# Moving TensorE's operands by 32 bytes, onto multiples of 256 bytes

## The chip, the core and the metric

The kernel runs on one core of a Trainium2 chip. A core has a matrix engine (TensorE, PE in the profile, with its weight loads shown apart as PEld), a vector engine (VectorE, DVE), a scalar engine (ScalarE, ACT), a general one (GpSimd, POOL), and a queue engine that issues most transfers (SyncE, SP). They share one on-chip memory of 128 partitions; a tile has the same byte range in every partition, and "byte 196,384" below is an offset within a partition. Matmul sums are gathered in a second memory, PSUM. The metric is the time on the device in microseconds, the median of several runs. Less is better.

A matmul here reads two operands from the on-chip memory. The *stationary* one, always 128 x 128, is loaded ahead by an instruction of its own (LDWEIGHTS, on PEld) while the matmul before it runs. The *moving* one is streamed through, a column at a time: 512, 288, 256 or 128 columns in this kernel.

## The reference

A sequence of 256 tokens of width 2,048 goes through two layers. Layer 0 mixes tokens with a convolution module, layer 1 with latent attention; each is followed by an MLP with squared ReLU.

```python
h = rms_norm(x, norm_mixer_g[layer])
# layer 0
u = h @ w_pw1 + b_pw1;  a, gate = split(u, 2);  u = a * sigmoid(gate)
u = causal depthwise conv of width 31 (u) + b_dw
x = x + silu(layer_norm(u)) @ w_pw2 + b_pw2
# layer 1
c_q, c_kv, k_pe = split(h @ w_in, [512, 1024])
q = rms_norm(c_q) @ w_q_up;  kv = rms_norm(c_kv) @ w_kv_up     # 16 heads
o = softmax(q k^T with rotary parts, block-causal mask) v
x = x + o @ w_o
# both
h = rms_norm(x, norm_mlp_g[layer])
x = x + square(relu(h @ w1)) @ w2                              # 2048 -> 8192 -> 2048
```

The output is a last `rms_norm` of x. Everything is in float32.

## The kernel before

Each float32 matrix is split into two parts, `hi` (rounded to the engine's reduced float32, F32R) and `lo` (the rest), and a product is the sum of three: hi by hi, hi by lo, lo by hi. ScalarE makes `hi` of a weight tile (line 170), VectorE, and in the convolution stage GpSimd, makes `lo` (line 174). Weights stream in through three `raw` tiles and six tiles each of `hi` and `lo`. The activations, turned so that their features lie along the partitions, are split in the same way.

What is stationary and what moves differs from stage to stage. In order of time:

1. **Convolution, first product** (`conv_mm`, line 823): for each of 16 channel blocks 96 matmuls with the weights (`hi`, `lo`) stationary and the turned input `xt` moving, 256 columns. Beside them VectorE does the taps of the depthwise convolution (line 910).
2. **Convolution, second product** (line 1287, then `mm3`, lines 203 to 205): the activations `sh`, `sl_` stationary, 512 columns of weights moving.
3. **MLP up** (lines 655 and 656), four stretches in all, two per layer: weights stationary, `xt` moving. The tile `xt` holds for each block of 128 features 256 columns of hi and then 256 of lo. Line 655 takes both (512 columns) against the weights' `hi`, line 656 the hi alone (256 columns) against the weights' `lo`; the two alternate.
4. **MLP down** (`mm3`): activations `gh`, `gl`, `sh`, `sl` stationary, 512 columns of weights moving. In the kernel's last product the last block of one row half is cut in two, with 256 columns each: 24 matmuls.
5. **Attention**, between the two MLPs: the products with `w_in` have `xt` stationary and 288 (keys and values) or 512 (queries) columns of weights moving. They give the compressed keys and values `kvh`, `kvl` and queries `qh`, `ql`. `k_piece` (lines 1535 to 1537) and `qn_piece` (1564 to 1566) have weights stationary and `kvh`, `kvl`, `qh`, `ql` moving, 256 columns; `v_piece` and `qp_piece` have those four stationary and 512 or 256 columns of weights moving. Scores, weights and values of each head follow on head tiles (`kTh`, `kTl`, `qTh`, `qTl`, `qpA`, `qpB`, `kpA`, `kpB`, `vv`, `pT`), then the product with `w_o` has the heads' outputs `oh`, `ol` stationary.

The order of the work is written out by hand, per engine, and every engine does its instructions in that order. Tiles lie where pools put them: pools on the left grow upward from the constants, one after the other, and the pools on the right side (`edge`, and above it `xt0`, `gp`, `xt1` or `gf` in turn) grow downward from the top. A tile's start therefore follows from the sizes of those below (or above) it, and a few unused tiles shift the rest:

```python
PAD_CONST = 8
PAD_SMALL = 48
PAD_RIGHT = 48
PAD_KV = 8
PAD_O = 56
```

`pad_right` lies at the top of the memory, ahead of `xt`; `pad_kv` ahead of attention's `kvh`; `pad_o` between the `qpB` tiles and `oh`. The start bytes that this gives, as the program is laid out, modulo 256:

```
tile                                    start byte before (mod 256)
hi, lo (split weights)                  46,080 (0), 70,656 (0), each next one 4,096 on
sh, sl, gh, gl (MLP), sh, sl_ (conv)    0
oh, ol                                  123,648 (0), 140,032 (0)
xt                                      196,384 (32), each next one 8,192 on
kvh, kvl, qh, ql                        96,800 (32) and on, 4,096 each
kpA, kpB, qpB                           113,184 (32) and on
kTh, kTl, qTh, qTl, qpA, vv, pT, gf     176,928 (32) and on
ident (for transposes)                  160
```

Within these tiles every operand of a matmul starts a multiple of 512 bytes on (128 columns of 4 bytes), but for the 288-column halves (1,152 bytes), so the number in brackets is that of the operand.

Of the kernel before, what the change touches and what calls it, by code (L numbers as in the profile page):

```python
# [10 lines left out]
F32 = mybir.dt.float32  # L11
# [7 lines left out]
P = 128  # L19
# [16 lines left out]
HALVES = 2  # L36
PAD_CONST = 8
PAD_SMALL = 48
PAD_RIGHT = 48
PAD_KV = 8  # L40
PAD_O = 56
WB = 6
LOOK = WB // 2 - 1
MIXED = {(layer, half): (0, 1, 4, 5, 8, 9, 12) + (13,) * (layer + half < 2) for layer in range(2) for half in range(2)}
# [35 lines left out]
def trunk_kernel(  # L80
# [26 lines left out]
    nc = tc.nc  # L107
# [26 lines left out]
    edge = ctx.enter_context(tc.tile_pool(name="edge", bufs=1, side="right"))  # L134
    pad_right = edge.tile([P, PAD_RIGHT], F32, name="pad_right")
    nc.gpsimd.memset(pad_right, 0.0)
# [179 lines left out]
    at, cols = 0, []  # L316
# [1053 lines left out]
    with ExitStack() as cx:  # L1370
        at = cx.enter_context(tc.tile_pool(name="at", bufs=1, reuse_waits="tile"))
# [91 lines left out]
                if h == 1:  # L1463
                    u_load(u + 3)

        pad_kv = at.tile([P, PAD_KV], F32, name="pad_kv")
        nc.gpsimd.memset(pad_kv, 0.0)
        kvh = at.tile([P, KR // P, S], F32R, name="kvh")
        kvl = at.tile([P, KR // P, S], F32R, name="kvl")
        qh = at.tile([P, QR // P, S], F32R, name="qh")  # L1470
# [18 lines left out]
            lambda i=i, j=j: nc.scalar.activation(qpB[i][DR:, j, :], mq[DR:, :], AF.Copy)  # L1489
            for i in range(2) for j in range(HG)  # L1490
        ]
        pad_o = at.tile([P, PAD_O], F32, name="pad_o")
        nc.gpsimd.memset(pad_o, 0.0)
        oh = at.tile([P, H, S], F32R, name="oh")
        ol = at.tile([P, H, S], F32R, name="ol")

# [447 lines left out]
```

## Time and profile before

| | |
|---|---|
| time, median of 3 runs | 1934.27 us (1934.19 to 1934.36) |
| span of the profiled execution | 1932.5 us |
| TensorE busy in it | 1921.0 us, 10,725 matmuls |
| VectorE, ScalarE, GpSimd busy | 1592.2, 1095.6, 249.0 us |

The profiled execution's span, from its first to its last instruction, is 1.8 us below the median of the runs; those 1.8 us lie around the span, outside what the trace shows. The profile's time of one matmul includes the way through the array, in which the next one has already begun. What a matmul costs in a row of them is the distance from its start to the next one's start; it is worked out below from rows of the timeline, whose first column is the start, or from a row with the first and last start of so many.

### The profile page before, as it was taken

The numbers are of one execution on the slowest core, as the hardware profiler recorded it, in microseconds if no ns is written. First come the engines' busy times: TensorE is split into PE (matmuls) and PEld (weight loads), VectorE is DVE, ScalarE is ACT, GpSimd is POOL, SyncE is SP. The second block draws the span as 40 slices with busy tenths as digits, with TensorE's granted clock in tenths as the row PEclk, the third lists the DMA queues.
The fourth block names the chain that finished last, engine by engine and source line by source line (L and its number), as shares of the span: only waits on it lengthen the run. The fifth ranks groups of instructions, "written<-read, shape, count | busy, mean of one in ns | idle before, by whom it ended". The sixth has DMA issues, their size and how long they took to land.

```text
span 1932.5 us, 28477 instructions
## 1 busy us (share of the span) xinstructions
PE 1921.0 (99%) x10725; PEld 1681.5 (87%) x10725; DVE 1592.2 (82%) x2457; ACT 1095.6 (57%) x1636; POOL 249.0 (13%) x208
## 2 busy tenths in 40 slices
PE   9999999999999999999999999999999999999998
PEld 8999888888888888888898998888888888888887
DVE  7999988877999776799976766877789987678998
ACT  5667755554555545555576655555555554455554
POOL 6999200000010100000001420000000010000000
PEclk9999999999999999999999999999999999999999
DMA  7766456665585866655656545465646776665774
GB/s 230 214 183 189 153 189 206 193 194 177 175 251 194 263 195 187 194 174 196 217 176 175 142 134 192 155 216 186 188 162 225 222 248 212 191 196 175 231 219 150
DMA packets 230427, 375.50 MB, mean 194 GB/s; under 512 B 16392, under 2 KB 107792, under 8 KB 230032
## 3 DMA queue, kind: packets, MB, share of 16 engines
q1 hardware_dynamic: 224640, 363.28, 58.7%
q0 software_dynamic: 4320, 7.87, 2.2%
q10 hardware_dynamic: 1328, 2.52, 0.4%
q8 instruction: 84, 1.38, 0.3%
q14 instruction: 55, 0.45, 0.1%
HBM read 363.68 MB, written 2.10 MB: 189 GB/s over the span
## 4 chain that ended last, share of the span: by engine, by line
PE 97%; DVE 2%; DMA 0%; ACT 0%; issue 0%; ACTq 0%; DVEq 0%
PE acc L655 24%; PE acc L205 15%; PE acc L203 15%; PE acc L204 15%; PE acc L656 13%; PE acc L823 8%; PE acc L1287 2%; DVE sum L910 1%; DMA xs<-in_x 0%; PE acc L1535 0%; PE acc L1566 0%; PE acc L1565 0%; PE acc L1536 0%; PE acc L1564 0%; PE acc L1537 0%; PE tr L267 0%
## 5 line engine op out<-in xcount | busy, mean ns | idle before, releaser
L174 DVE TENSOR_TENSOR lo<-raw,hi 128x1024 fp32r<-128x1024 f32 (+2 forms) x509 | 602.2, 1197 | 232.3 <-ACT hi L170 226.6
L170 ACT ACTIVATE hi<-raw 128x1024 fp32r<-128x1024 f32 (+2 forms) x574 | 583.9, 1036 | 361.1 <-PE acc L655 203.7
L655 PE MATMUL acc<-xt,hi 128*128 128x512 f32 x2048 | 710.6, 390 | 0.0
L656 PE MATMUL acc<-xt,lo 128*128 128x256 f32 x2048 | 577.5, 282 | 0.0
L655 PEld LDWEIGHTS acc<-xt,hi 128*128 128x128 f32 x2048 | 384.3, 188 | 80.7
L656 PEld LDWEIGHTS acc<-xt,lo 128*128 128x128 f32 x2048 | 387.1, 189 | 0.2
L497 ACT ACTIVATE hi<-raw 128x1024 fp32r<-128x1024 f32 x248 | 228.7, 948 | 228.3 <-DVE raw L505 134.0
L498 DVE TENSOR_TENSOR lo<-raw,hi 128x1024 fp32r<-128x1024 f32 x248 | 263.9, 1087 | 27.6 <-ACT hi L497 22.5
L203 PE MATMUL acc<-hi,sh 128*128 128x512 f32 x514 | 200.1, 389 | 0.0
L205 PE MATMUL acc<-lo,sh 128*128 128x512 f32 x514 | 200.1, 389 | 0.0
L203 PE MATMUL acc<-hi,gh 128*128 128x512 f32 (+1 forms) x516 | 200.0, 388 | 0.0
L205 PE MATMUL acc<-lo,gh 128*128 128x512 f32 (+1 forms) x516 | 199.9, 387 | 0.0
L204 PE MATMUL acc<-hi,gl 128*128 128x512 f32 (+1 forms) x516 | 199.9, 387 | 0.0
L823 PE MATMUL acc<-xt,hi 128*128 128x256 f32 x1024 | 180.2, 281 | 0.3 <-ACT b L1106 0.2
L204 PE MATMUL acc<-hi,sl 128*128 128x512 f32 x450 | 175.1, 389 | 0.0
L578 POOL DMA_DIRECT2D xs<-v x30 | 26.5, 994 | 1136.4 <-DVE lo L174 703.2
L910 DVE SCALAR_TENSOR_TENSOR sum<-ub,w_dw,sum 128x256 f32<-128x256 f32 x409 | 164.3, 481 | 3.6 <-ACT sum L880 3.0
L174 POOL TENSOR_TENSOR lo<-raw,hi 128x1024 fp32r<-128x1024 f32 x65 | 155.0, 2410 | 17.3 <-ACT hi L170 17.3
L823 PEld LDWEIGHTS acc<-xt,hi 128*128 128x128 f32 x1024 | 154.8, 188 | 1.1 <-ACT xt L1090 0.6
L823 PE MATMUL acc<-xt,lo 128*128 128x256 f32 x512 | 139.2, 279 | 0.0
L205 PEld LDWEIGHTS acc<-lo,sh 128*128 128x128 f32 x514 | 96.5, 188 | 20.4 <-DVE lo L498 0.3
L204 PEld LDWEIGHTS acc<-hi,gl 128*128 128x128 f32 x516 | 96.9, 188 | 19.9
(314 smaller groups left out, 2531.3 us busy)
## 6 DMA issues: line engine op xcount, KB each, us to landing
raw<-in_mlp_w SPq DMA_DIRECT2D x255, 1024.0 KB, 5.5
raw<-in_conv_w_pw SPq DMA_DIRECT2D x62, 512.0 KB, 5.1
raw<-in_conv_w_pw SPq DMA_DIRECT2D x16, 1024.0 KB, 5.1
raw<-in_mla_w_o SPq DMA_DIRECT2D x16, 1024.0 KB, 5.7
raw<-in_mla_w_kv_up SPq DMA_DIRECT2D x32, 256.0 KB, 3.9
xs<-v POOLq DMA_DIRECT2D x30, 256.0 KB, 7.8
raw<-in_mla_w_in SPq DMA_DIRECT2D x8, 576.0 KB, 3.8
raw<-in_mla_w_in SPq DMA_DIRECT2D x4, 1024.0 KB
```

Source lines behind the costliest of these rows:

```text
L170: nc.scalar.activation(hi, raw[:, js, :], AF.Copy)
L174: eng.tensor_tensor(lo, raw, hi.bitcast(F32), op=ALU.subtract)
L203: nc.tensor.matmul(ps, sh, mh, start=start, stop=False)
L204: nc.tensor.matmul(ps, sl, mh, start=False, stop=False)
L205: nc.tensor.matmul(ps, sh, ml, start=False, stop=stop)
L497: nc.scalar.activation(hi, src, AF.Copy)
L498: nc.vector.tensor_tensor(lo, src, hi.bitcast(F32), op=ALU.subtract)
L655: nc.tensor.matmul(ps[b], wh[:, bs], xhl(k), start=k == 0, stop=False)
L656: nc.tensor.matmul(ps[b][:, :S], wl[:, bs], xh(k), start=False, stop=k == KC - 1)
L823: nc.tensor.matmul(pss[c][b][:, :S], w[i][:, bs], (xh, xl)[j](k), start=k == i + j == 0, stop=end and k == k0 + nk - 1 and (i, j) == terms ...
L910: nc.vector.scalar_tensor_tensor(out=out, in0=ubs[c][:, w : w + S], scalar=tap(c, w), in1=base, op0=ALU.mult, op1=ALU.add)
L1287: nc.tensor.matmul(ps2[b][t], x_kt(k, t), w[:, bs], start=k == g == i == 0, stop=k == KC - 1 and i == len(group) - 1,)
```

## The change

The three unused tiles change, and nothing else. `pad_right` grows from 48 to 56 float32 per partition (192 to 224 bytes), so everything on the right side lies 32 bytes lower. `pad_kv` (32 bytes) goes, so attention's `kvh` up to `qpB1` lie 32 bytes lower. `pad_o` (224 bytes) goes too, so `oh`, `ol` and the tiles above them lie 256 bytes lower, with the same remainder as before. The memsets that filled the two tiles, on GpSimd, go with them.

```diff
-PAD_RIGHT = 48
-PAD_KV = 8
-PAD_O = 56
+PAD_RIGHT = 56
...
-        pad_kv = at.tile([P, PAD_KV], F32, name="pad_kv")
-        nc.gpsimd.memset(pad_kv, 0.0)
         kvh = at.tile([P, KR // P, S], F32R, name="kvh")
...
-        pad_o = at.tile([P, PAD_O], F32, name="pad_o")
-        nc.gpsimd.memset(pad_o, 0.0)
         oh = at.tile([P, H, S], F32R, name="oh")
```

After it, all tiles of the table above but `ident` start at a multiple of 256 bytes: `xt` at 196,352, `kvh` at 96,768, `kTh` at 176,896, `oh` at 123,392. On TensorE, VectorE, ScalarE and SyncE the same instructions stand in the same order as before; on GpSimd two of 212 are gone.

## The prediction

> **What bounds the kernel now.** I read the page first (busy shares, clock, chain), then the groups of instructions by shape, then starts in the timeline.
>
> ```profile
> PE 1921.0 (99%) x10725; PEld 1681.5 (87%) x10725; DVE 1592.2 (82%) x2457; ACT 1095.6 (57%) x1636; POOL 249.0 (13%) x208
> PEclk9999999999999999999999999999999999999999
> PE 97%; DVE 2%; DMA 0%; ACT 0%; issue 0%; ACTq 0%; DVEq 0%
> ```
>
> TensorE is busy 99% of the span, at full clock in every slice, and holds 97% of the chain that ended last. So the time is the number of matmuls times the distance between their starts. The change leaves the matmuls as they are and moves only the bytes that they read; it acts if that distance depends on where operands begin. The trace can tell, since operands begin at two places now, on a multiple of 256 bytes and 32 behind one.
>
> *512 columns, both operands on the multiple* (MLP down; first and last of 58 starts in a row):
>
> ```profile
> 599.78 0.39 PE L203 MATMUL acc<-hi,gh 128*128 128x512 f32 x1
> ...
> 612.70 0.39 PE L203 MATMUL acc<-hi,sh 128*128 128x512 f32 x1
> ```
>
> 12.92 us over 57 distances: 226.7 ns. *512 columns, stationary operand 32 behind* (`xt`, then `kvh`; 7 starts in a row, then 9):
>
> ```profile
> 1029.10 0.40 PE L204 MATMUL acc<-hi,xt 128*128 128x512 f32 x1
> ...
> 1030.50 0.40 PE L204 MATMUL acc<-hi,xt 128*128 128x512 f32 x1
> ...
> 1045.11 0.40 PE L204 MATMUL acc<-hi,kvl 128*128 128x512 f32 x1
> ...
> 1046.98 0.28 PE L203 MATMUL acc<-hi,qh 128*128 128x256 f32 x1
> ```
>
> 1.40 us over 6, 1.87 over 8: 233.3 and 233.8 ns, 7 more. *256 columns, moving operand 32 behind* (convolution, 96 matmuls to a piece of the chain; `kvh` in attention, 18 starts):
>
> ```profile
> 101.48 0.22 PE tr L969 x2
> 101.70 11.21 PE acc L823 x96
> 112.92 0.22 PE tr L969 x2
> 113.14 11.21 PE acc L823 x96
> ...
> 1034.91 0.28 PE L1535 MATMUL acc<-kvh,hi 128*128 128x256 f32 x1
> ...
> 1036.89 0.28 PE L1537 MATMUL acc<-kvh,lo 128*128 128x256 f32 x1
> ```
>
> 11.21 / 96 = 116.8 ns, and 1.98 / 17 = 116.5. *256 columns, both on the multiple*: only the 24 matmuls of the cut block at the end.
>
> ```profile
> 1921.70 0.28 PE L203 MATMUL acc<-hi,gh 128*128 128x256 f32 x1
> 1921.82 0.28 PE L204 MATMUL acc<-hi,gl 128*128 128x256 f32 x1
> 1921.93 0.28 PE L205 MATMUL acc<-lo,gh 128*128 128x256 f32 x1
> 1922.05 0.28 PE L203 MATMUL acc<-hi,gh 128*128 128x256 f32 x1
> ...
> 1924.45 0.28 PE L205 MATMUL acc<-lo,gh 128*128 128x256 f32 x1
> ```
>
> From 1922.05 on 20 distances take 2.40 us: 120.0 ns each. So what is 7 ns dearer at 512 columns off the multiple is 3.3 ns *cheaper* at 256. The mean times of the groups say the same without any arithmetic:
>
> ```profile
> L204 PE MATMUL acc<-hi,gl 128*128 128x512 f32 x508 | 197.7, 389 | 0.0
> L204 PE MATMUL acc<-hi,xt 128*128 128x512 f32 x32 | 12.7, 396 | 0.0
> L204 PE MATMUL acc<-hi,ol 128*128 128x512 f32 x128 | 50.0, 390 | 0.0
> L204 PE MATMUL acc<-hi,gl 128*128 128x256 f32 x8 | 2.3, 283 | 0.0
> L823 PE MATMUL acc<-xt,lo 128*128 128x256 f32 x512 | 139.2, 279 | 0.0
> ```
>
> Between the two aligned kinds, 256 columns cost 226.7 - 120.0 = 106.7 ns, 0.417 ns a column, which leaves 13.3 ns for each matmul whatever its length. I take that as the law of aligned operands: 13.3 ns and 0.417 ns a column.
>
> **The change part by part.**
>
> *MLP up, 2,048 pairs.* Today a pair (512 columns, then 256; both moving operands 32 behind) takes:
>
> ```profile
> L655 PE MATMUL acc<-xt,hi x448: 390/390/481, 322.7 to 477.7; 128*128 128x512 f32 x150
> L656 PE MATMUL acc<-xt,lo 128*128 128x256 f32 x2048 | 577.5, 282 | 0.0
> ```
>
> 155.0 us over 447 pairs: 346.8 ns. By the law it is 226.7 + 120.0 = 346.7 after. Term: 0. This is the largest lever by far, since 1 ns on a pair is 2.0 us, and no row shows an aligned alternation. Its bounds are two states 6.7 ns off. One is shorter: the first 256-column matmul behind 512-column ones, at 1921.70 above, and the two behind it take 0.35 us where three take 0.36, so a 256 that always follows a 512 might stay that short, 340 a pair. The other is longer, at the start of an up stretch:
>
> ```profile
> 300.31 0.40 PE L655 MATMUL acc<-xt,hi 128*128 128x512 f32 x1
> ...
> 301.37 0.39 PE L655 MATMUL acc<-xt,hi 128*128 128x512 f32 x1
> ```
>
> Three pairs in 1.06 us, 353 each, before they settle. Each bound is 6.7 x 2,048 = 13.7 us, down or up. I take 0, between them, where the law and today's row agree.
>
> *Convolution's first product.* 1,536 matmuls of 256 columns go from 116.7 to 120.0. Of the first block 40 wait for their input and don't count; its other 56 and the 15 x 96 of the blocks behind it run without a pause. That TensorE sets their pace needs a look, since VectorE is as full there:
>
> ```profile
> 20.13 6.54 PE acc L823 x56
> ...
> L823 PE MATMUL acc<-xt,hi 128*128 128x256 f32 x617 | 109.4, 280 | 0.0
> ACT sg L841 <- PE acc L823: 32.7, 10, 4.5
> L910 DVE SCALAR_TENSOR_TENSOR sum<-ub,w_dw,sum 128x256 f32<-128x256 f32 x261 | 104.8, 480 | 0.5
> ```
>
> From 60 to 170 us TensorE never idles, and it is ScalarE (line 841), which starts each channel block, that waits for TensorE, once a block. VectorE, nearly gapless, gets a little slack from a slower TensorE and takes none from it. So nothing hides the term: 1,496 x 3.3 ns = +4.9 us. The bounds are 0 (VectorE was the real pace) and 5.1.
>
> *Attention with 256 columns of `kvh`, `kvl`, `qh`, `ql` moving.* Six lines of 64, of which
>
> ```profile
> L1535 PE MATMUL acc<-kvh,hi 128*128 128x256 f32 x64 | 18.1, 282 | 0.0
> L1564 PE MATMUL acc<-qh,hi 128*128 128x256 f32 x64 | 18.1, 283 | 0.0
> ```
>
> are two: 384 x (120.0 - 116.5) = +1.3 us, with no idle time before them.
>
> *Stationary `xt` and `kvh` with 512 columns.* Three lines of 32 each for queries and values: 192 x (233.5 - 226.7) = -1.3 us. *Stationary `xt` with 288 columns*, 192 matmuls, 21 starts of which:
>
> ```profile
> 999.81 0.29 PE L204 MATMUL acc<-hi,xt 128*128 128x288 f32 x1
> ...
> 1002.46 0.29 PE L203 MATMUL acc<-hi,xt 128*128 128x288 f32 x1
> ```
>
> 132.5 ns now, 13.3 + 288 x 0.417 = 133.4 after: +0.2 us. The heads' scores and `qp_piece`, some 250 matmuls of 128 and 256 columns, could move by 3 ns either way, under 1 us; I take 0.
>
> *GpSimd's two memsets.* GpSimd is 13% busy, and the first of them only waits:
>
> ```profile
> POOL pad_kv L1467 <- DVE v L677: 175.0, 1, 175.0
> ```
>
> No matmul waits for it: 0. ScalarE's and VectorE's reads and writes of the moved tiles: no row tells a price, and outside the convolution they have idle time (57% and 82% busy), so a few ns each stay hidden; 0, below 0.5 us either way.
>
> *Sum*: 0 + 4.9 + 1.3 - 1.3 + 0.2 = +5.1 us on a span of 1932.5, 1937.6. With the 1.8 us around the span, which the change doesn't touch, and against the median of the runs: 1934.3 + 5.1 = 1939.4 us, slower by 0.26%.
>
> **The rivals.**
>
> *Where operands begin doesn't matter.* Then the rows above differ for another reason (stage, neighbours, tile strides), and the time stays 1934.3. The same result comes if VectorE is the pace of the convolution: +5.1 - 4.9 = 1934.5. Against it speaks that `ol`, aligned, in the same stage and on the same line as `xt`, has 390 where `xt` has 396. For it, that the 120 ns come from one place, 3 us long. The Trainium skill ("TensorE: Matmul & The Clock Gate", "Step-by-step: what each phase is for") states this rival as a rule: TensorE has two independent read ports, and loading the next weights takes nothing from the running matmul. By that rule the change does nothing; the 233.5 against 226.7 ns, with only the stationary operand moved, speak against it here.
>
> *Alignment frees the alternating pairs.* Mechanism: a weight load that runs beside 512 columns is finished early, and the short matmul behind it is spared half its 13.3 ns, as at 1921.70. It decides as soon as the pair falls by 2.5 ns, which pays for all other terms; at 340 the time is 1939.4 - 13.7 = 1925.7, faster. Against it: in a closed alternation what the short one saves the long one may pay back, and one place shows it.
>
> *Aligned pairs lock into the long state.* Both streams begin in step, and the 353 ns of the first three pairs last: 1939.4 + 13.7 = 1953.1. For it, all that differs in those pairs is how the two streams lie to one another; against it, the stretches leave this state after three pairs.
>
> **How the numbers follow.** My forecast gets 0.54, no effect (or VectorE as the pace) 0.17, the long state 0.15, freed pairs 0.14. About 0.2%, 3.9 us, is what a measurement of this kernel can tell from no change. Of my forecast's own range, 1937 to 1942, about 0.04 of chance lies inside 0.2%. Slower: 0.50 + 0.15 = 0.65; within: 0.17 + 0.04 = 0.21; faster: 0.14. The range from 1932 to 1954 holds all cases but the freed pairs and the tails.
>
> **What would show it.** In the profile after: line 823 at 120 ns a matmul, so pieces of 96 in 11.5 us instead of 11.21, and mean times of 282 to 283 instead of 279 and 280; `hi,xt` and `hi,kvl` with 512 columns at 389 instead of 396; pairs of lines 655 and 656 at 346.7. I am wrong if the pairs move at all, by 2.0 us a nanosecond, or if line 823 keeps its 11.21 us or VectorE shows idle time that TensorE did not give it.

## The result, and the profile after

The changed kernel takes 1953.22 us, median of 4 runs (1952.98 to 1953.47), against 1934.23 us before (1934.19 to 1934.36): a ratio of 1.0097, 95% interval 1.0085 to 1.0109. It is slower by 1%, 19.0 us. The prediction had 1939.4 us, in a range from 1932 to 1954; the time is that of its rival "aligned pairs lock into the long state", 1953.1 us, which had a chance of 0.15.

The page of the changed kernel (busy shares, then the heaviest groups of matmuls by shape; its lines 653, 654 and 821 are 655, 656 and 823 of the kernel before):

```profile
span 1951.5 us, 28475 instructions
PE 1939.2 (99%) x10725; PEld 1685.3 (86%) x10725; DVE 1594.0 (82%) x2457; ACT 1098.7 (56%) x1636; POOL 248.9 (13%) x206
...
PE acc L653 25%; PE acc L203 15%; PE acc L201 15%; PE acc L202 15%; PE acc L654 12%; PE acc L821 9%; PE acc L1285 2%; DMA xs<-in_x 0%; PE acc L1559 0%; PE acc L1530 0%; PE acc L1529 0%; PE acc L1558 0%; PE acc L1560 0%; PE acc L1531 0%; PE tr L265 0%; PE acc L1673 0%
...
L653 PE MATMUL acc<-xt,hi 128*128 128x512 f32 x2048 | 723.7, 399 | 0.0
L654 PE MATMUL acc<-xt,lo 128*128 128x256 f32 x2048 | 575.1, 281 | 0.0
```

TensorE is as full as before; the same 10,725 matmuls are busy 18.2 us longer. The mean time of the 512-column matmul of the MLP up products went from 390 to 399 ns. The place to look is a row of them, in the timeline (first column: start) of an up stretch of layer 0:

```profile
400.02 0.40 PE L653 MATMUL acc<-xt,hi 128*128 128x512 f32 x1
400.26 0.28 PE L654 MATMUL acc<-xt,lo 128*128 128x256 f32 x1
400.38 0.40 PE L653 MATMUL acc<-xt,hi 128*128 128x512 f32 x1
400.62 0.28 PE L654 MATMUL acc<-xt,lo 128*128 128x256 f32 x1
400.73 0.40 PE L653 MATMUL acc<-xt,hi 128*128 128x512 f32 x1
400.96 0.28 PE L654 MATMUL acc<-xt,lo 128*128 128x256 f32 x1
401.08 0.40 PE L653 MATMUL acc<-xt,hi 128*128 128x512 f32 x1
```

Three pairs take 1.06 us, and they are not alike: from start to start 0.36, 0.35 and 0.35 us, and then from the beginning again. To the nanosecond the trace has 361, 350 and 349, over and over, 353.3 on the mean, where before the pairs, once settled, had 346 or 347. Over whole stretches (the view of one line, with its count and its first and last start; first a stretch of layer 0, then the opening of layer 1, then the rest of that stretch):

```profile
L653 PE MATMUL acc<-xt,hi x512: 389/398/403, 649.8 to 830.4; 128*128 128x512 f32 x171
...
L653 PE MATMUL acc<-xt,hi x64: 389/391/461, 1253.8 to 1275.8; 128*128 128x512 f32 x64
...
L653 PE MATMUL acc<-xt,hi x448: 395/398/477, 1276.2 to 1434.3; 128*128 128x512 f32 x150
```

180.6 us over 511 pairs is 353.4 ns; 158.1 over 447 is 353.7. But the 64 pairs that open layer 1 take 22.0 over 63, 349, and their median of 391 ns for line 653 instead of 398 says that most of them ran at the old pace, with the operands at the very same remainders. That odd group is followed up below.

The convolution's first product, two pieces of the chain, and then, from the groups between 60 and 170 us, VectorE's taps beside it (their number, busy time and mean; idle time before them):

```profile
104.25 11.52 PE acc L821 x96
115.98 11.52 PE acc L821 x96
```

```profile
L908 DVE SCALAR_TENSOR_TENSOR sum<-ub,w_dw,sum 128x256 f32<-128x256 f32 x255 | 102.6, 486 | 3.0 <-ACT sum L878 3.0
```

11.52 / 96 = 120.0 ns a matmul, instead of 116.8, and VectorE idles 3.0 us where it idled 0.5.

Where the 19.0 us of the span come from: 31 of 32 groups of 64 pairs at 353.3 instead of 346.7, 1,984 x 6.6 = 13.1 us; the convolution's 1,496 unpaused matmuls 4.7 us (the first of them starts 0.45 us later than before, the last 5.1 us); from the last up group of layer 0 to the first of layer 1, with all of attention in between, 0.5 us (1253.8 - 830.4, against 1241.3 - 818.4 before); and the 0.45 us that had already come up ahead of those 1,496. That is 18.8 us.

### The profile page after: what moved, and what is told of

It reads as the page before. It is cut to its first block, busy times and chain, and to the rows that moved or that the text cites. A ratio compares the mean times of both kernels' runs of the same rounds, so it can differ in the third digit from the quotient of the medians.

```text
span 1951.5 us, 28475 instructions
## 1 busy us (share of the span) xinstructions
PE 1939.2 (99%) x10725; PEld 1685.3 (86%) x10725; DVE 1594.0 (82%) x2457; ACT 1098.7 (56%) x1636; POOL 248.9 (13%) x206
## 4 chain that ended last, share of the span: by engine, by line
PE 98%; DVE 1%; DMA 0%; ACT 0%; issue 0%; ACTq 0%; DVEq 0%
PE acc L653 25%; PE acc L203 15%; PE acc L201 15%; PE acc L202 15%; PE acc L654 12%; PE acc L821 9%; PE acc L1285 2%; DMA xs<-in_x 0%; PE acc L1559 0%; PE acc L1530 0%; PE acc L1529 0%; PE acc L1558 0%; PE acc L1560 0%; PE acc L1531 0%; PE tr L265 0%; PE acc L1673 0%
## 5 line engine op out<-in xcount | busy, mean ns | idle before, releaser
L653 PE MATMUL acc<-xt,hi 128*128 128x512 f32 x2048 | 723.7, 399 | 0.0
L821 PE MATMUL acc<-xt,hi 128*128 128x256 f32 x1024 | 184.8, 285 | 0.3 <-ACT b L1104 0.2
L201 PEld LDWEIGHTS acc<-hi,gh 128*128 128x128 f32 x516 | 96.9, 188 | 20.0
L203 PEld LDWEIGHTS acc<-lo,gh 128*128 128x128 f32 x516 | 96.9, 188 | 19.8
```

The source lines that it names most:

```text
L201: nc.tensor.matmul(ps, sh, mh, start=start, stop=False)
L203: nc.tensor.matmul(ps, sh, ml, start=False, stop=stop)
L653: nc.tensor.matmul(ps[b], wh[:, bs], xhl(k), start=k == 0, stop=False)
L821: nc.tensor.matmul(pss[c][b][:, :S], w[i][:, bs], (xh, xl)[j](k), start=k == i + j == 0, stop=end and k == k0 + nk - 1 and (i, j) == terms ...
```

## The experiments

Each kernel was timed beside the kernel before on the same chip (1934.2 to 1934.3 us). "Pair" is the mean distance from one 512-column matmul of the up products to the next, read from rows like those above; "conv" a 96-matmul piece divided by 96.

### Which tiles carry it

`xt_only` moves only what lies on the right side, `xt` and the head tiles. `kv_only` moves only `kvh` up to `qpB1`.

```diff
-PAD_RIGHT = 48
+PAD_RIGHT = 56
```

> Only the turned input xt and the head tiles on the right side move to the multiple of 256 (the 56-float pad); kvh, kvl, qh, ql, oh stay where they were. If xt carries the loss: convolution 120 ns a matmul (+5.1 us), pairs of lines 655 and 656 at 353 ns (+13.2), queries with xt stationary at 227 instead of 233 (-0.7): 1952 us. If the pairs' long state hangs on the whole layout, or on chance, and not on where xt lies, they stay at 347 and the time is about 1939.

```diff
-PAD_KV = 8
-PAD_O = 56
...
-        pad_kv = at.tile([P, PAD_KV], F32, name="pad_kv")
-        nc.gpsimd.memset(pad_kv, 0.0)
...
-        pad_o = at.tile([P, PAD_O], F32, name="pad_o")
-        nc.gpsimd.memset(pad_o, 0.0)
```

> The other half alone: kvh, kvl, qh, ql, kpA, kpB, qpB on the multiple of 256, xt and the head tiles 32 bytes behind it as before. 384 matmuls with kvh to ql moving from 116.5 to 120 ns (+1.3 us), 96 with kvh stationary from 233.8 to 227 (-0.6): 1934.9 us, the same within 0.2%. If the attention tiles matter more than that, 1938 or more.

`xt_only`: 1952.3 us (1949.6 to 1952.9), ratio 1.0091 (1.0076 to 1.0106). Of its groups the one of line 655, and a stretch of it:

```profile
L655 PE MATMUL acc<-xt,hi 128*128 128x512 f32 x2048 | 723.7, 399 | 0.0
```

```profile
L655 PE MATMUL acc<-xt,hi x512: 389/398/403, 650.1 to 830.6; 128*128 128x512 f32 x171
```

`kv_only`: 1935.3 us (1935.0 to 1936.1), ratio 1.0006 (0.9996 to 1.0016), with the pairs as before (group of line 653, the 655 of the kernel before) and `kvh` to `ql` at 120 ns (one of their lines, median 283 ns, where it was 280 with the operand 32 behind):

```profile
L653 PE MATMUL acc<-xt,hi 128*128 128x512 f32 x2048 | 710.6, 390 | 0.0
```

```profile
L1531 PE MATMUL acc<-kvh,lo x64: 280/283/283, 1034.9 to 1132.9; 128*128 128x256 f32 x64
```

So `xt` carries all but about 1 us, near the 0.7 us expected of the other half, and the two halves add up. (By its time alone `kv_only` can't be told from no change, since its interval takes in 1; in its trace 0.9 us arises between 1045 and 1150 us, in attention.)

### Own remainder, or distance between the operands

Two kernels keep the distance between the moving and the stationary operand and change where both lie: `all_at_32` has them both 32 behind a multiple of 256 (distance 0, as after the change), `all_32_on` has the weights at 32 and `xt` at 64 (distance 32, as before the change).

```diff
-PAD_CONST = 8
+PAD_CONST = 16
```

> Every tile on the left side moves up by 32 bytes (the first pad doubled), so the split weights hi and lo, and gh, gl, sh, sl, oh, ol lie 32 behind the multiple as xt does; kvh to ql at 64. If what counts is how the moving operand lies to the stationary one, both lie alike: 120 ns in the convolution, 353 a pair, 227 for 512 columns in the MLP down: 1952 us. If each operand's own remainder counts, 512 columns with a stationary operand at 32 take 233 instead of 227, some 3,000 matmuls, +20 us, and the convolution keeps 117: 1954 us or more, with the profile's rows telling which of the two it is.

```diff
-PAD_CONST = 8
+PAD_CONST = 16
-PAD_RIGHT = 48
+PAD_RIGHT = 40
```

> Everything 32 bytes on from where it lies in the kernel before: split weights, activations, heads' outputs at 32 behind a multiple of 256, xt, head tiles and kvh to ql at 64. Each operand's own remainder differs from before, the distance between moving and stationary is the same 32 everywhere. If only that distance counts, all is as before: 116.7 ns in the convolution, 346.7 a pair, 233 for 512 columns with kvh stationary, 1934.2 us. If xt at 64 is bad in itself, as in the run with xt alone at 64, 117 and 351, 1943 us.

`all_at_32`: 1953.5 us, ratio 1.010 (1.0079 to 1.012). `all_32_on`: 1937.2 us (1936.8 to 1938.8), ratio 1.0018 (1.0008 to 1.0027). A stretch of pairs and a piece of the convolution of each; first `all_at_32`:

```profile
L655 PE MATMUL acc<-xt,hi x447: 395/398/403, 330.8 to 488.4; 128*128 128x512 f32 x149
```

```profile
106.42 11.52 PE acc L823 x96
```

and `all_32_on`:

```profile
L655 PE MATMUL acc<-xt,hi x447: 390/390/394, 325.9 to 480.5; 128*128 128x512 f32 x149
```

```profile
104.55 11.21 PE acc L823 x96
```

353.4 and 120.0 ns; 346.6 and 116.8. The first has every operand off the multiple of 256 and behaves like the changed kernel, the second has `xt` elsewhere than the kernel before and behaves like it. So it is the distance between the two operands that the pace goes by here, not the multiple of 256 that the change aimed at; one common shift, 32 bytes, was tried. Moving `xt` also moves it against every other tile on the left side. That the partner that counts is the matmul's own stationary operand is borne out by `kv_only`, where `kvh` to `ql`, on the left side themselves, went to 120 ns at distance 0. The same holds for long matmuls: with both operands at 32, `all_at_32` does its MLP down products at 226.7 ns as the kernel before does with both at 0, so the 20 us that the other theory expected there do not come.

`all_32_on` is 2.9 us above the kernel before for another reason. The convolution's second block starts 2.7 us later than before, and that is nearly the whole difference at the end of the span; from there on the matmuls keep the old pace, or in a few blocks one within about 1 ns of it. At the opening its chain does not go along TensorE but along the first loads:

```profile
20.33 1.63 SPq L160
22.01 1.85 SPq L307
...
26.12 2.71 DMA stage<-in_mla_kv_norm_g
```

The small vectors land at 28.8 us, and the chain waits for them; in the kernel before TensorE had turned them by 27.2. Why the loads are later with their tiles 32 bytes on was not tried.

### Other distances

`xt` and the head tiles alone, 64, 128 and 224 (that is -32) behind the split weights.

```diff
-PAD_RIGHT = 48
+PAD_RIGHT = 40
```

> As before, but with xt and the head tiles 64 bytes behind a multiple of 256 instead of 32 (the pad at 40 floats). If only the remainder by 64 counts, this acts as the multiple itself: 120 ns in the convolution, 353 a pair, 1952 us. If the multiple of 256 counts, 64 acts as 32 does: 116.8 and 347, 1934 us. Anything between says that the distance itself counts.

```diff
-PAD_RIGHT = 48
+PAD_RIGHT = 24
```

> As before, with xt and the head tiles 128 bytes behind the split weights instead of 32. At 32 a pair takes 346.7 ns and a convolution matmul 116.7, at 0 353.2 and 119.9, at 64 351.1 and 117.1. If the two streams clash by a pattern of 64 bytes, 128 acts as 64 or 0 does, 351 to 353 a pair, 1943 to 1952 us. If only a start in step is bad and any distance heals it the more the longer it is, 347 or less, 1934 or less.

```diff
-PAD_RIGHT = 48
+PAD_RIGHT = 64
```

> As before, with xt and the head tiles 32 bytes ahead of a multiple of 256 instead of 32 behind one (224). If the distance counts and not its sign, or if the remainder by 64 counts, all is as before: 116.7 and 346.7 ns, 1934 us. If the moving stream must lie behind the stationary one, it acts as the multiple itself or worse, 1952 us.

1943.1 us (ratio 1.0047, 1.0031 to 1.0064), 1946.0 us (1.0061, 1.0038 to 1.0083) and 1943.1 us (1.0046, 1.003 to 1.0062). Two stretches each of 64, of 128 and of 224:

```profile
L655 PE MATMUL acc<-xt,hi x425: 392/397/398, 329.9 to 479.7; 128*128 128x512 f32 x142
L655 PE MATMUL acc<-xt,hi x509: 392/392/397, 644.7 to 822.0; 128*128 128x512 f32 x170
```

```profile
L655 PE MATMUL acc<-xt,hi x447: 387/396/477, 325.7 to 482.3; 128*128 128x512 f32 x149
L655 PE MATMUL acc<-xt,hi x499: 387/396/400, 646.6 to 821.5; 128*128 128x512 f32 x167
```

```profile
L655 PE MATMUL acc<-xt,hi x444: 392/397/402, 325.9 to 482.5; 128*128 128x512 f32 x148
L655 PE MATMUL acc<-xt,hi x504: 392/392/397, 646.8 to 821.2; 128*128 128x512 f32 x168
```

| distance | pair, the two stretches | conv | time |
|---|---|---|---|
| 0 (changed) | 353.4, 353.4 | 120.0 | 1953.2 |
| 32 (before) | 346.8, 346.6 | 116.8 | 1934.2 |
| 64 | 353.3, 349.0 | 117.8 (113.4 at first) | 1943.1 |
| 128 | 351.1, 351.1 | 118.6 | 1946.0 |
| 224 | 353.5, 346.7 | 118.4 | 1943.1 |

None of the simple rules fits: not the remainder by 64 (64 and 128 differ from 0 and from each other), not "the farther the better", and not the bare distance without its sign (224 is not 32). And at 64 and at 224 the same distance gives two paces in two stretches of one execution. It does so within a stretch too. At 64 the first group of the first stretch, ahead of the row shown above, still ran at 349:

```profile
L655 PE MATMUL acc<-xt,hi x63: 392/392/398, 300.7 to 322.3; 128*128 128x512 f32 x63
```

The first pair of the second group then takes some 0.08 us longer, and from it on the pace is 353.3; at 224 it goes from 346.7 to 353.2 at the same place. The distance alone doesn't decide it.

Rows of equal matmuls can have two paces as well. At 64 the convolution's matmuls from the second block to the middle of the fourth, and then whole pieces further on:

```profile
27.20 27.67 PE acc L823 x244
...
66.62 11.31 PE acc L823 x96
```

27.67 / 244 is 113.4 ns, the shortest pace that lasted for 256 columns in any kernel here, and 11.31 / 96 is 117.8. The pace changes at the two transposes in the middle of the fourth block. No kernel was tried that holds 113.4.

### The same addresses, two rhythms

`poke_after` and `poke_before` put one more 128-column transpose into each of the 32 groups of the up products, ahead of the matmul of the fourth column block that starts its sum; its result is overwritten. `poke_once` does so in the second group of each of the four stretches of the changed kernel alone.

```diff
                             for b in range(4):
                                 bs = slice(b * P, (b + 1) * P)
+                                if k == 0 and b == 3:
+                                    nc.tensor.transpose(ps[3][:, :P], ident, ident)
```

> The changed kernel with one more 128-column transpose of the identity at each of the 32 group starts of the MLP up stretches, ahead of the fourth column block's first matmul, whose sum then overwrites it; 32 x 0.2 us = 6 us dearer by itself. In the changed kernel one of the up stretches (the first 128 matmuls of layer 1, in which TensorE waits once) ran at 348 a pair and all others at 353. If the pairs can settle in several rhythms at the same addresses, and a disturbance chooses, some of the 32 groups settle at 347 or below and others stay at 353 or so. If the addresses alone set the pace, all groups keep 353 but for a pair or two behind the transpose.

> The kernel before with the same 32 transposes, the control. Its pairs start at 353 in an up stretch and settle at 346.7 within three. If 346.7 is the only rhythm at a distance of 32 bytes, every group comes back to it and the time is 1934.2 + at most 8 us for the transposes and the settling. If a disturbance chooses there too, some groups stay at 353.

```diff
+                                if g == 1 and k == 0 and b == 3:
+                                    nc.tensor.transpose(ps[3][:, :P], ident, ident)
```

> The changed kernel with the extra transpose only at the second group of each of the four up stretches. If a disturbance picks the rhythm and the rhythm then lasts until the next one, each stretch runs from there to its end in one rhythm: at 346.7 where the transpose picked that (as behind the second group's transpose in three of four stretches with all 32), 7 groups of 64 pairs x 6.6 ns = 3.0 us each: 1953.2 - 9 = 1944 us, 1941 if all four do. If the rhythm falls back to 353 by itself, 1953 us.

`poke_after`: 1950.6 us, 2.7 below the changed kernel in spite of 32 more instructions. `poke_before`: 1938.0 us, 3.8 above the kernel before. `poke_once`: 1947.7 us, 5.5 below the changed kernel. The third and the fourth group of `poke_after`:

```profile
L654 PE MATMUL acc<-xt,hi x56: 391/391/391, 352.9 to 371.9; 128*128 128x512 f32 x56
L654 PE MATMUL acc<-xt,hi x54: 395/398/403, 375.9 to 394.6; 128*128 128x512 f32 x54
```

19.0 / 55 = 345 and 18.7 / 53 = 353, from starts rounded to 0.1 us: within one row of the view the median equals the extremes, or the times run from 395 to 403. Pair by pair, 16 of the 32 groups settle at 346.7 and 16 at 353.3 to 353.5. The outcome isn't drawn anew each time: through the first two stretches the groups settle at 353, 346.7, 346.7, 353 and then the same four again. In `poke_before` all 32 come back to 346.7. In `poke_once` two stretches change over at the second group and stay there; the other two don't change. The rest of the second stretch, and the first:

```profile
L654 PE MATMUL acc<-xt,hi x444: 392/395/475, 672.8 to 826.5; 128*128 128x512 f32 x148
...
L654 PE MATMUL acc<-xt,hi x442: 395/398/487, 328.9 to 484.8; 128*128 128x512 f32 x148
```

346.9 and 353.5. Two stretches of 7 groups, 14 x 64 x 6.6 ns = 5.9 us, make up the gain of `poke_once`, where three stretches were expected. So at distance 0 the alternation has more than one rhythm that keeps itself up, and a disturbance of a tenth of a microsecond can change it; at distance 32 every disturbance led back to 346.7.

That fits the odd group that opens layer 1 in the changed kernel: there TensorE waits once, at the group's fourth column block, and comes out in the other rhythm. But such a wait doesn't settle it. In `poke_once` the same group has the same wait (the 461 ns, as in the changed kernel's row) and stays at 353, which takes 0.4 us off the gain:

```profile
L654 PE MATMUL acc<-xt,hi x63: 389/398/461, 1250.7 to 1272.7; 128*128 128x512 f32 x63
```

And in the changed kernel a first pair that is 0.08 us longer, at the second group of two stretches, doesn't make the rest leave 353. What a disturbance must hit to change the rhythm stays open.

### The alternation taken apart

For each block of 128 features first the four 512-column matmuls, then the four of 256, in the kernel before (`fours_before`) and in the changed one (`fours_after`).

```diff
                                 nc.tensor.matmul(ps[b], wh[:, bs], xhl(k), start=k == 0, stop=False)
+                            for b in range(4):
+                                bs = slice(b * P, (b + 1) * P)
                                 nc.tensor.matmul(ps[b][:, :S], wl[:, bs], xh(k), start=False, stop=k == KC - 1)
```

> The kernel before, with the up product's alternation taken apart: for each block of 128 features first the four 512-column matmuls of line 655, then the four of 256 columns, xt still 32 behind. If short and long matmuls each keep the distance they have in a row of their kind, and a long one with the moving operand behind costs what it costs now, 228 + 116.7 = 344.7 a pair, 2,048 x -2.0 ns = -4 us: 1930 us, faster than both. If a long one off the multiple costs 233 as with the stationary operand behind, 350 a pair: +6.8 us, 1941 us.

> The changed kernel with the same order of fours. Without an alternation the law of aligned operands, which the pairs broke, should hold within each four: 4 x 226.7 + 3 x 120 + 113 = 1380 ns, 345 a pair instead of 353.2, 2,048 x -8.2 = -16.8 us: 1936 us. If aligned streams have a long state of their own, 353 a pair, it stays at 1953.

`fours_before`: 1944.1 us (1943.3 to 1944.7), ratio 1.0049 (1.0033 to 1.0066), slower. `fours_after`: 1951.0 us, ratio 1.0086 (1.0066 to 1.0106). Two rounds of four of `fours_before`:

```profile
399.69 1.09 PE L654 MATMUL acc<-xt,hi 128*128 128x512 f32 x4
400.63 0.63 PE L657 MATMUL acc<-xt,lo 128*128 128x256 f32 x4
401.09 1.09 PE L654 MATMUL acc<-xt,hi 128*128 128x512 f32 x4
402.03 0.63 PE L657 MATMUL acc<-xt,lo 128*128 128x256 f32 x4
```

A round takes 1.40 us, 350 a pair: 0.94 us for four long ones, 231 to 235 each, and 0.46 for four short ones, 116.7. `fours_after`, its first round in a stretch and a later one:

```profile
305.43 1.07 PE L652 MATMUL acc<-xt,hi 128*128 128x512 f32 x4
306.33 0.64 PE L655 MATMUL acc<-xt,lo 128*128 128x256 f32 x4
...
399.88 1.09 PE L652 MATMUL acc<-xt,hi 128*128 128x512 f32 x4
400.81 0.64 PE L655 MATMUL acc<-xt,lo 128*128 128x256 f32 x4
```

The first four long ones take 0.90 us, 226 to 227 each, as the law of aligned operands has it. The later ones take 0.93, with 224 to 236 each, and a pair 350.8: the law (345 expected) fails here too. So in rows of four the long ones end up near 233 at either distance (in a stretch's first round `fours_before` takes 0.94 us where `fours_after` takes 0.90), and these two kernels don't show that the distance of 32 is what makes them dear. What they do show is that at distance 32 the alternation, at 346.7, is better than fours. No version beat the kernel before.

## Why the prediction came out as it did

**What bounds the kernel**: right. TensorE is 99% busy before and after, and 18.2 of the 19.0 us are matmul time.

**The four prices read from the trace before**: right where a row of one kind runs. Convolution: 120.0 ns forecast from the 24 matmuls at the end, 120.0 measured, +4.9 us forecast, +4.7 measured; VectorE hid none of it and got slack (0.5 to 3.0 us idle). `kvh` to `ql` moving: 120 ns as forecast, in `kv_only` too. The term of -1.3 us for stationary tiles was too large: line 202 with `xt` and 512 columns fell from 396 to 390, but with `kvl` only from 395 to 392. Before, then after:

```profile
L204 PE MATMUL acc<-hi,kvl 128*128 128x512 f32 x32 | 12.6, 395 | 0.0
```

```profile
L202 PE MATMUL acc<-hi,xt 128*128 128x512 f32 x32 | 12.5, 390 | 0.0
L202 PE MATMUL acc<-hi,kvl 128*128 128x512 f32 x32 | 12.5, 392 | 0.0
```

Together with the rest, attention came to about +0.5 us where +0.2 had been summed up.

**The time itself**: "slower" came out right, but only 5 of the 19 us came from the terms that the forecast of +5.1 us was summed from. The range held the time because a rival's bound was in it, not because of the forecast.

**MLP up, term 0**: this step failed, and it was the largest. "I take that as the law of aligned operands" carried two prices from rows of one kind into an alternation of two kinds, 226.7 + 120.0 = 346.7. An aligned alternation doesn't add up like that: it ran at 353.3 in 31 of 32 groups, +13.1 us. The bound had been seen and priced, from the three pairs that open a stretch, at 353 and +13.7 us; what was wrong was to give it 0.15 because "the stretches leave this state after three pairs". They leave it at distance 32. At distance 0 the rhythm lasts. That the rival's time fits to 0.1 us is partly luck: its 353 was the mean of 354, 353 and 352 ns, three pairs on their way to 346.7, while the lasting rhythm goes 361, 350, 349 and every stretch opens with a single pair of 340. The two have the mean in common; that they are one state isn't shown.

**The rival "where operands begin doesn't matter"** is out: `xt_only` alone costs 18 us with no other change. The rule by which the change does nothing, which the prediction cites from the Trainium skill ("TensorE: Matmul & The Clock Gate", "Step-by-step: what each phase is for"), doesn't give the time of this kernel. What counts is where one operand begins relative to the other, which the prediction's wording ("on the multiple", "32 behind one") did not separate from each operand's own remainder; `all_at_32` and `all_32_on` do.

**The rival "alignment frees the pairs"**: 340 a pair lasted in no stretch of any kernel; single pairs of it open stretches of the changed kernel, with 350 and 361 right behind them.

What stays open: why these distances give these rhythms. That the moving stream and the weight load disturb each other as they run side by side would fit, but no run separated the two or showed what they clash over.

## What to carry to other kernels

Where a kernel is bound by back-to-back matmuls, look at the distance between the starting bytes of what moves and what is loaded beside it, stage by stage: 32 bytes were worth 1% here, and for this kernel as a whole a round alignment of everything was the worst of the distances tried. A price read from a row of equal matmuls doesn't carry over to an alternation, so measure the alternation itself, over whole stretches. When identical code at identical distances shows two paces, look for a rhythm that a wait or an extra instruction starts, before explaining either by the code.

## What the runs showed of the hardware

Start to start, matmuls of 512 and 256 columns in turn have several lasting rhythms, by the distance of their operands: 346.7 and 353.3 ns a pair at distance 0, 349 and 353.3 at 64, 346.7 and 353.2 at 224; at 32 only 346.7 was seen to last, and at 128 only 351.1. Each is kept for whole groups of 64 pairs, mostly for hundreds of pairs, and where the pace changed within a stretch, a start was 0.06 to 0.1 us late or a transpose stood in between. Not every late start changed it. Rows of 256-column matmuls have more than one pace too: 120.0 ns at distance 0, 116.7 at 32 with some blocks at 117.8, 113.4 and then 117.8 at 64.
